# Instance norm in 3D on one core: three 64 KiB slots loaded, then three stored, in turn on one queue, with a two-pass variance split over the engines

## Chip, cores, metric

One Trainium2 chip (trn2), one of its cores. The metric is device time in microseconds (us), the median of several runs. The profile comes from one execution; its span is about 1.7 us shorter than the timed run (1249.7 against about 1251.5 us before).

Engines are named as the profile names them: PE is TensorE, DVE is VectorE, ACT is ScalarE, POOL is GpSimd, SP is SyncE. SP does no arithmetic here: it issues every load and store, one after another.

## The reference

```python
batch, channels, d, h, w = 8, 64, 32, 64, 64        # x is drawn from a standard normal, float32
def reference(x, eps):                              # eps = 1e-5
    mean = np.mean(x, axis=(2, 3, 4), keepdims=True)
    var = np.var(x, axis=(2, 3, 4), keepdims=True)
    return ((x - mean) / np.sqrt(var + eps)).astype(np.float32)
```

There are 512 instances of 131,072 elements. The kernel has to read 268.44 MB and write 268.44 MB; each element needs a statistic first and a multiply and an add afterwards.

## The kernel before

A tile holds 8 instances, each over 16 partitions, so 128 partitions x 8192 columns (32 KiB a partition, 4 MiB). Four such tiles exist. Statistics take one pass: DVE sums the values while ACT sums the squares. A small matmul adds up the 16 partitions of each instance. The normalise is split over three engines, in place.

```python
LAG = 2
data_pool = ctx.enter_context(tc.tile_pool(name="data", bufs=4))
# ... cut
norm_splits = [(nc.vector, 0, c1), (nc.scalar, c1, c2), (nc.gpsimd, c2, F)]   # c1 = F // 8, c2 = F // 4
# ... cut: in issue_compute, for each tile
nc.vector.reduce_sum(out=psums[:, k, 0:1], in_=x_tiles[:, k, :], axis=mybir.AxisListType.X)
nc.scalar.activation(out=sq_scratch, in_=x_tiles[:, k, :],
                     func=mybir.ActivationFunctionType.Square, accum_out=psums[:, k, 1:2])
# ... cut: matmul, mean, E[x^2] - mean^2, sqrt, reciprocal, bias, then the three normalise pieces
pending = {}
for g in range(n_groups):
    x_tiles = issue_load(g)
    issue_compute(g, x_tiles)
    pending[g] = x_tiles
    if g >= LAG:
        issue_store(g - LAG, pending.pop(g - LAG))
for g in range(n_groups - LAG, n_groups):
    issue_store(g, pending.pop(g))
```

Loads and stores therefore alternate in SP's program, and store g-2 stands behind load g.

Of the kernel before, what the change touches and what calls it, by code (L numbers as in the profile page):

```python
# [1 line left out]

# [4 lines left out]


@with_exitstack
def kernel(  # L10
    ctx: ExitStack,
    tc: tile.TileContext,
    x: bass.AP,
    eps: bass.AP,
    out: bass.AP,
):
    nc = tc.nc
    fp32 = mybir.dt.float32

    P = 128  # L20
    B, C, D, H, W = x.shape
    n_inst = B * C
    n_elem = D * H * W

    eps_f = float(eps)

    SPLIT = 16
    IPT = P // SPLIT
    F = n_elem // SPLIT

    G = 8
    KPG = G // IPT
    n_groups = n_inst // G

    LAG = 2

    x_packed = x.rearrange("b c d h w -> (b c) (d h w)").rearrange(
        "(k i) (s f) -> k (i s) f", i=IPT, s=SPLIT
    )
    out_packed = out.rearrange("b c d h w -> (b c) (d h w)").rearrange(  # L40
        "(k i) (s f) -> k (i s) f", i=IPT, s=SPLIT
    )

    singles = ctx.enter_context(tc.tile_pool(name="singles", bufs=1))
    data_pool = ctx.enter_context(tc.tile_pool(name="data", bufs=4))
    scratch_pool = ctx.enter_context(tc.tile_pool(name="scratch", bufs=2))
    stat_pool = ctx.enter_context(tc.tile_pool(name="stats", bufs=4))
    psum_pool = ctx.enter_context(tc.tile_pool(name="psum", bufs=4, space=bass.MemoryType.PSUM))

    ones_t = singles.tile([P, P], fp32)  # L50
    nc.vector.memset(ones_t, 1.0 / SPLIT)  # L51
    blk_pattern = [[-SPLIT, P // SPLIT], [0, SPLIT]]
    nc.gpsimd.affine_select(  # L53
        out=ones_t,
        in_=ones_t,
        pattern=blk_pattern,
        compare_op=mybir.AluOpType.is_ge,
        fill=0.0,
        base=0,
        channel_multiplier=1,  # L60
    )
    nc.gpsimd.affine_select(  # L62
        out=ones_t,
        in_=ones_t,
        pattern=[[SPLIT, P // SPLIT], [0, SPLIT]],
        compare_op=mybir.AluOpType.is_ge,
        fill=0.0,
        base=SPLIT - 1,
        channel_multiplier=-1,
    )  # L70

    inv_F = 1.0 / F

    c1 = F // 8
    c2 = F // 4
    norm_splits = [
        (nc.vector, 0, c1),
        (nc.scalar, c1, c2),
        (nc.gpsimd, c2, F),
    ]  # L80

    def issue_load(g):
        x_tiles = data_pool.tile([P, KPG, F], fp32, name="x_tiles")
        src = x_packed[g * KPG : (g + 1) * KPG].rearrange("k p f -> p k f")
        nc.sync.dma_start(out=x_tiles, in_=src)
        return x_tiles

    def issue_compute(g, x_tiles):
        psums = stat_pool.tile([P, KPG, 2], fp32, name="psums")

        for k in range(KPG):
            nc.vector.reduce_sum(  # L92
                out=psums[:, k, 0:1],
                in_=x_tiles[:, k, :],
                axis=mybir.AxisListType.X,
            )
            sq_scratch = scratch_pool.tile(
                [P, F], mybir.dt.bfloat16, name="sq_scratch"
            )
            nc.scalar.activation(  # L100
                out=sq_scratch,
                in_=x_tiles[:, k, :],
                func=mybir.ActivationFunctionType.Square,
                accum_out=psums[:, k, 1:2],
            )

        tot = psum_pool.tile([P, KPG, 2], fp32, name="tot")
        nc.tensor.matmul(  # L108
            out=tot,
            lhsT=ones_t,  # L110
            rhs=psums,
            start=True,
            stop=True,
        )

        me2 = stat_pool.tile([P, KPG, 2], fp32, name="me2")
        nc.vector.tensor_scalar(  # L117
            out=me2,
            in0=tot,
            scalar1=inv_F,  # L120
            scalar2=None,
            op0=mybir.AluOpType.mult,
        )
        mean = me2[:, :, 0]
        e2 = me2[:, :, 1]

        msq = stat_pool.tile([P, KPG], fp32, name="msq")
        nc.vector.tensor_mul(out=msq, in0=mean, in1=mean)  # L128

        var_eps = stat_pool.tile([P, KPG], fp32, name="var_eps")  # L130
        nc.vector.scalar_tensor_tensor(  # L131
            out=var_eps,
            in0=e2,
            scalar=eps_f,
            in1=msq,
            op0=mybir.AluOpType.add,
            op1=mybir.AluOpType.subtract,
        )

        std = stat_pool.tile([P, KPG], fp32, name="std")  # L140
        nc.scalar.activation(  # L141
            out=std,
            in_=var_eps,
            func=mybir.ActivationFunctionType.Sqrt,
        )
        scale = stat_pool.tile([P, KPG], fp32, name="scale")
        nc.vector.reciprocal(out=scale, in_=std)  # L147
        bias = stat_pool.tile([P, KPG], fp32, name="bias")
        nc.vector.scalar_tensor_tensor(  # L149
            out=bias,  # L150
            in0=mean,
            scalar=-1.0,
            in1=scale,
            op0=mybir.AluOpType.mult,
            op1=mybir.AluOpType.mult,
        )

        for k in range(KPG):
            for eng, lo, hi in norm_splits:
                if eng is nc.scalar:  # L160
                    nc.scalar.activation(  # L161
                        out=x_tiles[:, k, lo:hi],
                        in_=x_tiles[:, k, lo:hi],
                        func=mybir.ActivationFunctionType.Identity,
                        scale=scale[:, k : k + 1],
                        bias=bias[:, k : k + 1],
                    )
                else:
                    eng.tensor_scalar(  # L169
                        out=x_tiles[:, k, lo:hi],  # L170
                        in0=x_tiles[:, k, lo:hi],
                        scalar1=scale[:, k : k + 1],
                        scalar2=bias[:, k : k + 1],
                        op0=mybir.AluOpType.mult,
                        op1=mybir.AluOpType.add,
                    )

    def issue_store(g, x_tiles):
        dst = out_packed[g * KPG : (g + 1) * KPG].rearrange("k p f -> p k f")
        nc.sync.dma_start(out=dst, in_=x_tiles)  # L180

    pending = {}
    for g in range(n_groups):
        x_tiles = issue_load(g)
        issue_compute(g, x_tiles)
        pending[g] = x_tiles
        if g >= LAG:
            issue_store(g - LAG, pending.pop(g - LAG))
    for g in range(n_groups - LAG, n_groups):
        issue_store(g, pending.pop(g))  # L190


# [1 line left out]
_INS = ['x', 'eps']  # L194
_OUTS = [((8, 64, 32, 64, 64), 'float32')]
#: Inputs that are plain numbers.
_NUMBERS = {'eps': 9.999999747378752e-06}


# [26 lines left out]
```

## Time and profile before

| what | before |
|---|---|
| time, median of the first three runs (range) | 1251.46 us (1250.81 to 1252.0) |
| span of the profile | 1249.7 us |
| DMA queue's share of 16 engines' span; mean rate | 99.7%; 430 GB/s |
| busiest compute engine | DVE, 53% |
| DMA data packets (trace) | 16,384 of 32 KiB; median 1.213 us each |

First the page's engine line (busy us, share of the span, instruction count), its row of DMA shares in 40 slices of 31 us with the GB/s below it, and the line of the DMA queue (packets, MB, share of 16 engines). Read the digits as tenths of full occupation.

```profile
PE 35.7 (3%) x128; PEld 32.1 (3%) x128; DVE 659.2 (53%) x449; ACT 550.6 (44%) x258; POOL 380.3 (30%) x70
DMA  9999999999999999999999999999999999999998
GB/s 403 417 434 434 427 433 430 432 435 430 429 432 434 432 435 429 434 433 434 434 431 433 431 434 434 435 430 432 434 433 436 429 433 434 433 434 435 429 433 357
q1 hardware_dynamic: 18432, 536.88, 99.7%
```

No slice but the last falls below 9, and no compute engine is over 53%: the DMA engines bound this kernel from end to end. The Trainium skill ("DMA: Bandwidth & Descriptors", section "Where 436 GB/s comes from") gives 435 GB/s as the ceiling of the 16 ports through which the DMA engines reach on-chip memory; the slices, at 427 to 436 from the third to the last but one, agree. The same section goes on to say that transfers between the chip's main memory (HBM) and on-chip memory are held to about 358 GB/s; this trace does not agree: one core alone moved 430 GB/s in the mean. A saving in compute is worth nothing here, and compute that delays a transfer costs its whole delay.

The durations used for costing come from the page's groups of instructions (line, engine, operation, tile and shape, count | total busy us, mean ns of one | idle time before, and what ended it):

```profile
L92 DVE TENSOR_REDUCE psums<-x_tiles 128x1 f32<-128x8192 f32 x64 | 555.9, 8686 | 492.9 <-DMA x_tiles<-in_x_dram 492.9
L100 ACT ACTIVATE sq_scratch<-x_tiles 128x8192 bf16<-128x8192 f32 x64 | 449.9, 7029 | 461.3 <-DMA x_tiles<-in_x_dram 461.3
L169 POOL TENSOR_SCALAR x_tiles<-x_tiles,scale,bias 128x6144 f32<-128x6144 f32 x64 | 379.4, 5929 | 855.4 <-DVE bias L149 634.4
L161 ACT ACTIVATE x_tiles<-x_tiles,bias,scale 128x1024 f32<-128x1024 f32 x64 | 79.4, 1241 | 40.5 <-DVE bias L149 40.5
L169 DVE TENSOR_SCALAR x_tiles<-x_tiles,scale,bias 128x1024 f32<-128x1024 f32 x64 | 52.1, 813 | 2.5
```

DVE and ACT sit idle about 490 and 460 us in front of their statistics, waiting for loads: that is what slack looks like in a DMA-bound kernel.

One detail needs the instructions in order of time (start us, duration us, engine, line, operation). It shows how DVE's and POOL's shares of one normalise stand to each other:

```profile
1191.83 0.81 DVE L169 TENSOR_SCALAR x_tiles<-x_tiles,scale,bias 128x1024 f32<-128x1024 f32 x1
1192.04 5.93 POOL L169 TENSOR_SCALAR x_tiles<-x_tiles,scale,bias 128x6144 f32<-128x6144 f32 x1 [13.43 <-DVE bias L149]
...
1211.18 0.81 DVE L169 TENSOR_SCALAR x_tiles<-x_tiles,scale,bias 128x1024 f32<-128x1024 f32 x1
...
1211.70 5.63 POOL L169 TENSOR_SCALAR x_tiles<-x_tiles,scale,bias 128x6144 f32<-128x6144 f32 x1 [13.72 <-DVE bias L149]
```

POOL starts at different distances from DVE's start (0.21 and 0.52 us) and has different durations, but it ends 5.33 and 5.34 us after DVE *ends* (1191.83 + 0.81 = 1192.64, and 1192.04 + 5.93 = 1197.97). So POOL's work really begins when DVE's is over. The skill says the same ("SBUF — State Buffer", section "Who interferes with whom": a DVE instruction in a two-port mode, which takes the ports that the two engines share, and a GpSimd instruction exclude each other for the whole instruction). In this kernel it is harmless. When sizes change it has to be costed as a sum, not as a maximum.

### The profile page before, as it was taken

How to read it: one execution, taken by the hardware profiler on the slowest of the kernel's cores; microseconds unless marked ns; L12 is line 12 of the kernel's file. 1: busy time of each engine (PE TensorE's matmuls, PEld its weight loads, DVE VectorE, ACT ScalarE, POOL GpSimd, SP SyncE). 2: the span in 40 equal slices, each digit the busy share in tenths (PEclk: the TensorE clock that was granted, in tenths of full speed). 3: DMA queues.
4: the chain of work that ended last, by engine and by line, in shares of the span. 5: the costliest groups of instructions: out<-in, count | busy, mean ns of one | idle time of the engine just before them, and what ended most of it. 6: DMA issues, size and time to landing. Idle time of an engine off the chain costs nothing.

```text
span 1249.7 us, 1827 instructions
## 1 busy us (share of the span) xinstructions
PE 35.7 (3%) x128; PEld 32.1 (3%) x128; DVE 659.2 (53%) x449; ACT 550.6 (44%) x258; POOL 380.3 (30%) x70
## 2 busy tenths in 40 slices
PE   0000000000000000000000000000000000000000
PEld 0000000000000000000000000000000000000000
DVE  5736455464554645546546455464554645646543
ACT  5535445354453544535435344354453544534432
POOL 2332332313323233232331322313323233132231
DMA  9999999999999999999999999999999999999998
GB/s 403 417 434 434 427 433 430 432 435 430 429 432 434 432 435 429 434 433 434 434 431 433 431 434 434 435 430 432 434 433 436 429 433 434 433 434 435 429 433 357
DMA packets 18444, 536.99 MB, mean 430 GB/s; under 512 B 2048, under 2 KB 2048, under 8 KB 2048
## 3 DMA queue, kind: packets, MB, share of 16 engines
q1 hardware_dynamic: 18432, 536.88, 99.7%
q14 instruction: 11, 0.09, 0.0%
q8 instruction: 1, 0.02, 0.0%
HBM read 268.44 MB, written 268.44 MB: 430 GB/s over the span
## 4 chain that ended last, share of the span: by engine, by line
DMA 74%; issue 16%; POOL 7%; DVE 1%; POOLq 1%; PE 0%; ACT 0%
DMA out_dram<-x_tiles 39%; DMA x_tiles<-in_x_dram 35%; POOL x_tiles L169 7%; DVE psums L92 1%; POOLq L221 0%; DVE x_tiles L169 0%; POOLq L169 0%; PE tot L108 0%; ACT std L141 0%; DVE scale L147 0%; DVE msq L128 0%; DVE me L117 0%; DVE bias L149 0%; DVE var_eps L131 0%
## 5 line engine op out<-in xcount | busy, mean ns | idle before, releaser
L92 DVE TENSOR_REDUCE psums<-x_tiles 128x1 f32<-128x8192 f32 x64 | 555.9, 8686 | 492.9 <-DMA x_tiles<-in_x_dram 492.9
L100 ACT ACTIVATE sq_scratch<-x_tiles 128x8192 bf16<-128x8192 f32 x64 | 449.9, 7029 | 461.3 <-DMA x_tiles<-in_x_dram 461.3
L169 POOL TENSOR_SCALAR x_tiles<-x_tiles,scale,bias 128x6144 f32<-128x6144 f32 x64 | 379.4, 5929 | 855.4 <-DVE bias L149 634.4
L161 ACT ACTIVATE x_tiles<-x_tiles,bias,scale 128x1024 f32<-128x1024 f32 x64 | 79.4, 1241 | 40.5 <-DVE bias L149 40.5
L141 ACT ACTIVATE std<-var_eps 128x1 f32<-128x1 f32 x64 | 13.0, 203 | 178.7 <-DVE var_eps L131 178.7
L108 PE MATMUL tot<-psums,ones_t 128*128 128x2 f32 x128 | 35.7, 348 | 1193.5 <-DVE psums L92 1193.5
L108 PEld LDWEIGHTS tot<-psums,ones_t 128*128 128x128 f32 x128 | 32.1, 311 | 1197.1 <-issue 1197.1
L169 DVE TENSOR_SCALAR x_tiles<-x_tiles,scale,bias 128x1024 f32<-128x1024 f32 x64 | 52.1, 813 | 2.5
L117 DVE TENSOR_SCALAR me<-tot 128x2 f32<-128x2 f32 x64 | 10.2, 160 | 47.5 <-PE tot L108 47.5
L147 DVE RECIPROCAL scale<-std 128x1 f32<-128x1 f32 x64 | 10.5, 164 | 21.8 <-ACT std L141 21.8
L100 ACT ACTIVATION_READ_ACCUMULATOR sq_scratch<-x_tiles 128x1 f32 x64 | 11.9, 187 | 0.0
L128 DVE TENSOR_TENSOR msq<-me 128x1 f32<-128x1 f32 x64 | 10.2, 159 | 2.2
L131 DVE SCALAR_TENSOR_TENSOR var_eps<-me,msq 128x1 f32<-128x1 f32 x64 | 10.2, 159 | 2.2
L149 DVE SCALAR_TENSOR_TENSOR bias<-me,scale 128x1 f32<-128x1 f32 x64 | 10.2, 159 | 2.2
L100 ACT ACT_TABLE_LOAD x1 | 1.3, 1283 | 0.8 <-PEq L207 0.8
L141 ACT ACT_TABLE_LOAD x1 | 1.3, 1283 | 0.0
L51 DVE MEMSET ones_t<- 128x128 f32 x1 | 0.2, 165 | 0.9 <-PEq L207 0.9
L53 POOL TENSOR_SCALAR_AFFINE_SELECT ones_t<-ones_t 128x128 f32<-128x128 f32 x1 | 0.3, 343 | 0.6 <-DVE ones_t L51 0.6
L62 POOL TENSOR_SCALAR_AFFINE_SELECT ones_t<-ones_t 128x128 f32<-128x128 f32 x1 | 0.3, 338 | 0.1
L207 POOL MEMSET const-float32-0.0<- 128x1 f32 x1 | 0.1, 98 | 0.3 <-issue 0.3
L207 POOL MEMSET const-bfloat16-1.0<- 128x1 bf16 x1 | 0.1, 101 | 0.0
L207 POOL MEMSET const-uint8-127<- 128x1 uint8 x1 | 0.1, 101 | 0.0
(1 smaller groups left out, 0.1 us busy)
## 6 DMA issues: line engine op xcount, KB each, us to landing
x_tiles<-in_x_dram SPq DMA_DIRECT2D x64, 4096.0 KB, 29.0
out_dram<-x_tiles SPq DMA_DIRECT2D x64, 4096.0 KB, 31.5
```

Of the source, the lines that this page charges most:

```text
L92: nc.vector.reduce_sum(out=psums[:, k, 0:1], in_=x_tiles[:, k, :], axis=mybir.AxisListType.X,)
L100: nc.scalar.activation(out=sq_scratch, in_=x_tiles[:, k, :], func=mybir.ActivationFunctionType.Square, accum_out=psums[:, k, 1:2],)
L108: nc.tensor.matmul(out=tot, lhsT=ones_t, rhs=psums, start=True, stop=True,)
L117: nc.vector.tensor_scalar(out=me2, in0=tot, scalar1=inv_F, scalar2=None, op0=mybir.AluOpType.mult,)
L128: nc.vector.tensor_mul(out=msq, in0=mean, in1=mean)
L131: nc.vector.scalar_tensor_tensor(out=var_eps, in0=e2, scalar=eps_f, in1=msq, op0=mybir.AluOpType.add, op1=mybir.AluOpType.subtract,)
L141: nc.scalar.activation(out=std, in_=var_eps, func=mybir.ActivationFunctionType.Sqrt,)
L147: nc.vector.reciprocal(out=scale, in_=std)
L149: nc.vector.scalar_tensor_tensor(out=bias, in0=mean, scalar=-1.0, in1=scale, op0=mybir.AluOpType.mult, op1=mybir.AluOpType.mult,)
L161: nc.scalar.activation(out=x_tiles[:, k, lo:hi], in_=x_tiles[:, k, lo:hi], func=mybir.ActivationFunctionType.Identity, scale=scale[:, k : ...
L169: eng.tensor_scalar(out=x_tiles[:, k, lo:hi], in0=x_tiles[:, k, lo:hi], scalar1=scale[:, k : k + 1], scalar2=bias[:, k : k + 1], op0=mybir ...
L207: nc = _bacc.Bacc("TRN2", target_bir_lowering=False, num_devices=1)
```

## The change

The intent: bigger packets (64 KiB rows), transfers of one direction batched (three loads, then three stores), and a numerically safer variance (mean first, then the squares of x - mean), with the added pass spread over the engines. The data now lies in three slots of 128 x 16384 (8 MiB each, 24 MiB in all) instead of four of 4 MiB (16 MiB). The first two slots are loaded and stored in halves, so that work can begin early.

```diff
+    SLOTS = 3
+    COLS = 16384
+    BIG = P * COLS // n_elem        # 16 instances a slot
+    HALF = BIG // 2
# ... cut
+    def compute(t, n):
+        avg = avgs[n]
+        width = t.shape[1]
+        cut = width * 5 // 8
+        sums = stat_pool.tile([P, 2], fp32, name="sums")
+        nc.vector.reduce_sum(out=sums[:, 0:1], in_=t[:, :cut], axis=mybir.AxisListType.X)
+        accumulate(t[:, cut:], Act.Identity, 0.0, sums[:, 1:2])      # ACT sums the other 3/8
+        mean_ps = averaged(avg, sums, "mean_ps")
+        neg_mean = stat_pool.tile([P, 1], fp32, name="neg_mean")
+        nc.vector.tensor_scalar(out=neg_mean, in0=mean_ps, scalar1=-1.0, scalar2=None, op0=Alu.mult)
+        squares = stat_pool.tile([P, 2], fp32, name="squares")
+        used = accumulate(t, Act.Square, neg_mean, squares)          # 2 pieces of 8192 on ACT
+        var_ps = averaged(avg, squares[:, :used], "var_ps")
# ... cut: sqrt on ACT, reciprocal and bias on DVE
+        half, rest = width // 2, width * 3 // 4
+        nc.scalar.activation(out=t[:, rest:], in_=t[:, rest:], func=Act.Identity, scale=scale, bias=bias)
+        for engine, lo, hi in ((nc.gpsimd, 0, half), (nc.vector, half, rest)):
+            engine.tensor_scalar(out=t[:, lo:hi], in0=t[:, lo:hi], scalar1=scale, scalar2=bias,
+                                 op0=Alu.mult, op1=Alu.add)
# ... cut
+    loaded, stored = 0, 0
+    while stored < n_slots:
+        load_and_compute(range(loaded, min(stored + SLOTS, n_slots)))
+        loaded = min(stored + SLOTS, n_slots)
+        turn = first_turn if stored == 0 else SLOTS
+        for g in range(stored, stored + turn):
+            for part in work.pop(g):
+                store(*part)
+        stored += turn
```

The diff does not show how ACT's instructions of different slots end up interleaved; the built program does. In a full turn of slots a, b, c, ACT runs: sum a, squares a, **sum b**, sqrt a, normalise a, squares b, **sum c**, sqrt b, normalise b, squares c, sqrt c, normalise c.

More of the change, by code (lines that the diff above doesn't have):

```diff
@@ L4 @@
 import concourse.tile as tile
-from concourse import bass_utils, mybir
+from concourse import mybir
 from concourse._compat import with_exitstack
@@ L18 @@
     fp32 = mybir.dt.float32
+    Alu = mybir.AluOpType
+    Act = mybir.ActivationFunctionType
     P = 128
@@ L25 @@
     eps_f = float(eps)
-    SPLIT = 16
-    IPT = P // SPLIT
-    F = n_elem // SPLIT
-    G = 8
-    KPG = G // IPT
-    n_groups = n_inst // G
-    LAG = 2
-    x_packed = x.rearrange("b c d h w -> (b c) (d h w)").rearrange(
-        "(k i) (s f) -> k (i s) f", i=IPT, s=SPLIT
-    )
-    out_packed = out.rearrange("b c d h w -> (b c) (d h w)").rearrange(
-        "(k i) (s f) -> k (i s) f", i=IPT, s=SPLIT
-    )
-    singles = ctx.enter_context(tc.tile_pool(name="singles", bufs=1))
-    data_pool = ctx.enter_context(tc.tile_pool(name="data", bufs=4))
@@ L46 @@
-    scratch_pool = ctx.enter_context(tc.tile_pool(name="scratch", bufs=2))
-    stat_pool = ctx.enter_context(tc.tile_pool(name="stats", bufs=4))
-    psum_pool = ctx.enter_context(tc.tile_pool(name="psum", bufs=4, space=bass.MemoryType.PSUM))
-    ones_t = singles.tile([P, P], fp32)
-    nc.vector.memset(ones_t, 1.0 / SPLIT)
-    blk_pattern = [[-SPLIT, P // SPLIT], [0, SPLIT]]
-    nc.gpsimd.affine_select(
-        out=ones_t,
-        in_=ones_t,
-        pattern=blk_pattern,
-        compare_op=mybir.AluOpType.is_ge,
-        fill=0.0,
-        base=0,
-        channel_multiplier=1,
-    )
@@ L62 @@
-    nc.gpsimd.affine_select(
-        out=ones_t,
-        in_=ones_t,
-        pattern=[[SPLIT, P // SPLIT], [0, SPLIT]],
-        compare_op=mybir.AluOpType.is_ge,
-        fill=0.0,
-        base=SPLIT - 1,
-        channel_multiplier=-1,
-    )
-    inv_F = 1.0 / F
-    c1 = F // 8
-    c2 = F // 4
-    norm_splits = [
-        (nc.vector, 0, c1),
-        (nc.scalar, c1, c2),
-        (nc.gpsimd, c2, F),
-    ]
-    def issue_load(g):
-        x_tiles = data_pool.tile([P, KPG, F], fp32, name="x_tiles")
-        src = x_packed[g * KPG : (g + 1) * KPG].rearrange("k p f -> p k f")
-        nc.sync.dma_start(out=x_tiles, in_=src)
-        return x_tiles
@@ L88, in issue_compute @@
-    def issue_compute(g, x_tiles):
-        psums = stat_pool.tile([P, KPG, 2], fp32, name="psums")
-        for k in range(KPG):
-            nc.vector.reduce_sum(
-                out=psums[:, k, 0:1],
-                in_=x_tiles[:, k, :],
-                axis=mybir.AxisListType.X,
-            )
-            sq_scratch = scratch_pool.tile(
-                [P, F], mybir.dt.bfloat16, name="sq_scratch"
-            )
-            nc.scalar.activation(
-                out=sq_scratch,
-                in_=x_tiles[:, k, :],
-                func=mybir.ActivationFunctionType.Square,
-                accum_out=psums[:, k, 1:2],
-            )
-        tot = psum_pool.tile([P, KPG, 2], fp32, name="tot")
-        nc.tensor.matmul(
-            out=tot,
-            lhsT=ones_t,
-            rhs=psums,
-            start=True,
-            stop=True,
-        )
-        me2 = stat_pool.tile([P, KPG, 2], fp32, name="me2")
-        nc.vector.tensor_scalar(
-            out=me2,
-            in0=tot,
-            scalar1=inv_F,
-            scalar2=None,
-            op0=mybir.AluOpType.mult,
-        )
-        mean = me2[:, :, 0]
-        e2 = me2[:, :, 1]
-        msq = stat_pool.tile([P, KPG], fp32, name="msq")
-        nc.vector.tensor_mul(out=msq, in0=mean, in1=mean)
-        var_eps = stat_pool.tile([P, KPG], fp32, name="var_eps")
-        nc.vector.scalar_tensor_tensor(
-            out=var_eps,
-            in0=e2,
-            scalar=eps_f,
-            in1=msq,
-            op0=mybir.AluOpType.add,
-            op1=mybir.AluOpType.subtract,
-        )
-        std = stat_pool.tile([P, KPG], fp32, name="std")
-        nc.scalar.activation(
-            out=std,
-            in_=var_eps,
-            func=mybir.ActivationFunctionType.Sqrt,
-        )
-        scale = stat_pool.tile([P, KPG], fp32, name="scale")
-        nc.vector.reciprocal(out=scale, in_=std)
-        bias = stat_pool.tile([P, KPG], fp32, name="bias")
-        nc.vector.scalar_tensor_tensor(
-            out=bias,
-            in0=mean,
-            scalar=-1.0,
-            in1=scale,
-            op0=mybir.AluOpType.mult,
-            op1=mybir.AluOpType.mult,
-        )
-        for k in range(KPG):
-            for eng, lo, hi in norm_splits:
-                if eng is nc.scalar:
-                    nc.scalar.activation(
-                        out=x_tiles[:, k, lo:hi],
-                        in_=x_tiles[:, k, lo:hi],
-                        func=mybir.ActivationFunctionType.Identity,
-                        scale=scale[:, k : k + 1],
-                        bias=bias[:, k : k + 1],
-                    )
-                else:
-                    eng.tensor_scalar(
-                        out=x_tiles[:, k, lo:hi],
-                        in0=x_tiles[:, k, lo:hi],
-                        scalar1=scale[:, k : k + 1],
-                        scalar2=bias[:, k : k + 1],
-                        op0=mybir.AluOpType.mult,
-                        op1=mybir.AluOpType.add,
-                    )
@@ L178, in issue_store @@
-    def issue_store(g, x_tiles):
-        dst = out_packed[g * KPG : (g + 1) * KPG].rearrange("k p f -> p k f")
-        nc.sync.dma_start(out=dst, in_=x_tiles)
-    pending = {}
-    for g in range(n_groups):
-        x_tiles = issue_load(g)
-        issue_compute(g, x_tiles)
-        pending[g] = x_tiles
-        if g >= LAG:
-            issue_store(g - LAG, pending.pop(g - LAG))
-    for g in range(n_groups - LAG, n_groups):
-        issue_store(g, pending.pop(g))
+    SLOTS = 3
+    COLS = 16384
@@ new lines, with averaging @@
+    BIG = P * COLS // n_elem
+    HALF = BIG // 2
+    x_f = x.rearrange("b c d h w -> (b c) (d h w)")
+    out_f = out.rearrange("b c d h w -> (b c) (d h w)")
+    singles = ctx.enter_context(tc.tile_pool(name="singles", bufs=1))
+    data_pool = ctx.enter_context(tc.tile_pool(name="data", bufs=SLOTS))
+    stat_pool = ctx.enter_context(tc.tile_pool(name="stats", bufs=4))
+    psum_pool = ctx.enter_context(
+        tc.tile_pool(name="psum", bufs=2, space=bass.MemoryType.PSUM)
+    )
+    def averaging(split):
+        avg = singles.tile([P, P], fp32, name=f"avg{split}")
+        nc.vector.memset(avg, 1.0 / n_elem)
+        nc.gpsimd.affine_select(
+            out=avg,
+            in_=avg,
+            pattern=[[-split, P // split], [0, split]],
+            compare_op=Alu.is_ge,
+            fill=0.0,
+            base=0,
+            channel_multiplier=1,
+        )
+        nc.gpsimd.affine_select(
+            out=avg,
+            in_=avg,
+            pattern=[[split, P // split], [0, split]],
+            compare_op=Alu.is_ge,
+            fill=0.0,
+            base=split - 1,
+            channel_multiplier=-1,
+        )
+        return avg
@@ new lines, with rows, load, store @@
+    avgs = {n: averaging(P // n) for n in (HALF, BIG)}
+    eps_t = singles.tile([P, 1], fp32, name="eps_t")
+    nc.vector.memset(eps_t, eps_f)
+    unused = singles.tile([P, COLS // 2], mybir.dt.uint8, name="unused")
+    def rows(ap, first, n):
+        return ap[first : first + n].rearrange("i (s f) -> (i s) f", s=P // n)
+    def load(t, first, n):
+        nc.sync.dma_start(out=t, in_=rows(x_f, first, n))
+    def store(t, first, n):
+        nc.sync.dma_start(out=rows(out_f, first, n), in_=t)
@@ new lines, in accumulate, with averaged @@
+    def accumulate(t, func, bias, to):
+        width = t.shape[1]
+        pieces = -(-width // unused.shape[1])
+        step = width // pieces
+        for k in range(pieces):
+            nc.scalar.activation(
+                out=unused[:, :step],
+                in_=t[:, k * step : (k + 1) * step],
+                func=func,
+                bias=bias,
+                accum_out=to[:, k : k + 1],
+            )
+        return pieces
+    def averaged(avg, parts, name):
+        ps = psum_pool.tile([P, 1], fp32, name=name)
+        n = parts.shape[1]
+        for k in range(n):
+            nc.tensor.matmul(
+                out=ps,
+                lhsT=avg,
+                rhs=parts[:, k : k + 1],
+                start=k == 0,
+                stop=k == n - 1,
+            )
+        return ps
@@ new lines, in compute @@
+    def compute(t, n):
+        avg = avgs[n]
+        width = t.shape[1]
+        cut = width * 5 // 8
+        sums = stat_pool.tile([P, 2], fp32, name="sums")
+        nc.vector.reduce_sum(
+            out=sums[:, 0:1], in_=t[:, :cut], axis=mybir.AxisListType.X
+        )
+        accumulate(t[:, cut:], Act.Identity, 0.0, sums[:, 1:2])
+        mean_ps = averaged(avg, sums, "mean_ps")
+        neg_mean = stat_pool.tile([P, 1], fp32, name="neg_mean")
+        nc.vector.tensor_scalar(
+            out=neg_mean, in0=mean_ps, scalar1=-1.0, scalar2=None, op0=Alu.mult
+        )
+        squares = stat_pool.tile([P, 2], fp32, name="squares")
+        used = accumulate(t, Act.Square, neg_mean, squares)
+        var_ps = averaged(avg, squares[:, :used], "var_ps")
+        std = stat_pool.tile([P, 1], fp32, name="std")
+        nc.scalar.activation(out=std, in_=var_ps, func=Act.Sqrt, bias=eps_t)
+        scale = stat_pool.tile([P, 1], fp32, name="scale")
+        nc.vector.reciprocal(out=scale, in_=std)
+        bias = stat_pool.tile([P, 1], fp32, name="bias")
+        nc.vector.tensor_mul(out=bias, in0=neg_mean, in1=scale)
+        half, rest = width // 2, width * 3 // 4
+        nc.scalar.activation(
+            out=t[:, rest:], in_=t[:, rest:], func=Act.Identity, scale=scale, bias=bias
+        )
+        for engine, lo, hi in ((nc.gpsimd, 0, half), (nc.vector, half, rest)):
+            engine.tensor_scalar(
+                out=t[:, lo:hi],
+                in0=t[:, lo:hi],
+                scalar1=scale,
+                scalar2=bias,
+                op0=Alu.mult,
+                op1=Alu.add,
+            )
@@ new lines, with load_and_compute @@
+    n_slots = n_inst // BIG
+    first_turn = n_slots % SLOTS or SLOTS
+    work = {}
+    def load_and_compute(group):
+        for g in group:
+            t = data_pool.tile([P, COLS], fp32, name="xt")
+            if g < first_turn:
+                cut = COLS // 2
+                work[g] = [
+                    (t[:, :cut], g * BIG, HALF),
+                    (t[:, cut:], g * BIG + HALF, HALF),
+                ]
+            else:
+                work[g] = [(t, g * BIG, BIG)]
+            for part in work[g]:
+                load(*part)
+        for g in group:
+            for t, _, n in work[g]:
+                compute(t, n)
```

## The prediction

> **What bounds the kernel now.** The DMA engines. The DMA queue table gives q1 99.7% of 16 engines' span, 430 GB/s mean. The trace's DMA packets: 16,384 of 32 KiB, 1.213 us each in both directions (also in the all-load start and the all-store tail), so 1024 x 1.213 = 1242 us per engine. The busiest compute engine, DVE, is at 53%. The Trainium skill ("DMA: Bandwidth & Descriptors", "Where 436 GB/s comes from") puts the ceiling at 435 GB/s; the trace agrees. Bytes do not change, so the floor stays 536.9 MB / 435 = 1234 us.
>
> **What the change can save.** If a 64 KiB row is one packet, half the packets at about 8 ns overhead each: about 4 us. Batching directions saves nothing: packets take the same in both. No-bubble time: about 1243.
>
> **What it costs.** Before, loads and stores alternate, compute well ahead of the store. Now SP issues L L L, S S S per turn. A store waits for its compute, and no load can be queued meanwhile (SP is in order, all three slots are full). An 8 MiB transfer takes about 19.35 us, so after the first load of a turn lands (t=0) its store is due at 38.4, the next at 58, the third at 77.
>
> Durations scaled from the instruction groups of before: reduce of 10240 on DVE 10.8 (8.69 for 8192); ACT partial sum of 6144 5.5; squares 2 x 7.4 (7.03 + 0.19 accumulator read + 0.2 bias operand); ACT normalise of 4096 3.8; matmul pairs 0.7 to 1.3; sqrt, reciprocal, bias 0.65. Normalise: DVE 2.4, then POOL 7.05: before, each POOL normalise ends 5.34 us after DVE's, whenever it started. The skill agrees ("SBUF — State Buffer", "Who interferes with whom": DVE in a 2-port mode and GpSimd exclude each other). So 9.5.
>
> The built order on ACT is: sum a, squares a, sum b, sqrt a, normalise a, squares b, sum c, sqrt b, normalise b, squares c, sqrt c. Hence:
> - a: mean at 12.2, squares to 27.2, sum b to 32.7, bias 33.4, normalised 43.0. Due 38.4; with 0.85 us from issue to first packet (last store of before): gap 5.5.
> - b: squares 37.2 to 52.0, sum c to 57.5, normalised 67.9; first packet 68.7, store a ended 63.2: gap 5.5.
> - c: squares 62.0 to 76.8, normalised 87.7; store b ends 88.1: gap about 0.4.
>
> About 11.4 us of idle DMA per turn, on the critical path because the DMA queue is empty then. Nine full turns give 103 us; the first, short turn about 6, its half stores being hidden behind the third load. 1243 + 103 + 6, about 1350 us.
>
> **Prediction: 1350 us, 80% range 1325 to 1375; faster 0.01, same 0.05, slower 0.94.**
>
> **What would show each step.** Packets about 9,500, of 64 KiB, 2.42 us each. DMA queue share about 92%, mean about 398 GB/s; slices dip twice per turn, between last load and first store and between first and second store. SP's waits: stores on POOL or DVE normalise for 4 to 5 us after the DMA ran dry. The chain of waits goes through ACT squares and sums instead of DMA alone. ACT busy about 780 us, DVE about 450.
>
> **What would make it wrong.** DVE and POOL normalising side by side (only gap a shrinks; ACT sets b); sum b not delaying sqrt a; pure-direction phases moving faster than 435 GB/s, which no stretch of the trace shows; extra semaphore waits between ACT's squares (slower).

## The result

| what | before | after |
|---|---|---|
| time, median of 4 runs (range) | 1251.73 us (1250.81 to 1252.65) | 1351.16 us (1351.05 to 1351.32) |
| ratio, 95% interval | | 1.0795 (1.0779 to 1.081): slower |
| span of the profile | 1249.7 us | 1349.6 us |
| DMA queue's share; mean rate | 99.7%; 430 GB/s | 92.7%; 398 GB/s |
| 16 DMA engines idle between first and last packet, mean of the engines | 4.2 us | 97.0 us |
| packets' own time, per engine | 1245.3 us | 1250.8 us |
| of which slow packets, per engine | 3.2 us | 12.5 us |

Ratios are the mean time of one kernel's fast runs over that of the other's of the same rounds, so not quite the ratio of the medians. The last three rows are worked out from the start and duration of every DMA packet in the trace: idle is the time in which fewer than 16 packets are in flight, weighted by the missing ones; slow packets are the sum of what each packet takes beyond the median of its size (1.213 us for 32 KiB, 2.418 us for 64 KiB), divided by 16.

The change costs 99.4 us (1351.16 - 1251.73). In the profiled pair, whose spans differ by 99.9 us, engine idle time accounts for 92.8 and the packets' own time for 5.5; the last 2 us I don't attribute.

The same lines of the page as before; the slices are 34 us long here:

```profile
PE 73.8 (5%) x264; PEld 64.5 (5%) x264; DVE 453.1 (34%) x173; ACT 764.7 (57%) x266; POOL 295.2 (22%) x42
DMA  9999899889988998899799889988998899699979
GB/s 404 422 448 435 373 404 435 373 373 404 435 373 373 421 429 361 373 435 435 305 410 435 373 373 404 435 373 373 404 435 373 371 435 431 286 435 412 396 342 404
q1 hardware_dynamic: 9792, 536.88, 92.7%
```

The busiest compute engine, ACT, is at 57%. By this line alone everything would still be hidden behind the DMA. But the DMA row now has 7s and 8s (and one 6) all the way along, and the GB/s row falls to 373 or below twice in nearly every turn, that is in about two slices of four. The average of busy time says nothing about *when* ACT is busy.

The groups that answer to those of before. A line's mean may mix two shapes: these are the views by shape, so it doesn't.

```profile
L88 ACT ACTIVATE unused<-xt,neg_mean 128x8192 uint8<-128x8192 f32 x64 | 455.5, 7117 | 78.7 <-DVE neg_mean L122 77.7
L116 DVE TENSOR_REDUCE sums<-xt 128x1 f32<-128x10240 f32 x30 | 324.6, 10820 | 551.9 <-DMA xt<-in_x_dram 551.9
L139 POOL TENSOR_SCALAR xt<-xt,scale,bias 128x8192 f32<-128x8192 f32 x30 | 276.4, 9214 | 978.3 <-DVE bias L133 856.0 <-ACT std L129 75.9 <-DVE neg_mean L122 46.4
L88 ACT ACTIVATE unused<-xt 128x6144 uint8<-128x6144 f32 x30 | 159.7, 5323 | 441.4 <-DMA xt<-in_x_dram 440.8
L135 ACT ACTIVATE xt<-xt,bias,scale 128x4096 f32<-128x4096 f32 x30 | 114.1, 3802 | 15.6 <-issue 9.4 <-DVE bias L133 6.2
```

POOL's mean of 9.2 us for 8192 columns is not its speed: in most of these instructions the first 2.4 us are a wait for DVE.

Now one full turn in order of time. Slot a lands at 732.40, b at 751.75, c at about 771.

```profile
732.40 5.32 ACT L88 ACTIVATE unused<-xt 128x6144 uint8<-128x6144 f32 x1 [46.74 <-DMA xt<-in_x_dram]
732.40 10.82 DVE L116 TENSOR_REDUCE sums<-xt 128x1 f32<-128x10240 f32 x1 [48.21 <-DMA xt<-in_x_dram]
...
744.57 7.12 ACT L88 ACTIVATE unused<-xt,neg_mean 128x8192 uint8<-128x8192 f32 x1 [6.76 <-DVE neg_mean L122]
...
751.82 7.12 ACT L88 ACTIVATE unused<-xt,neg_mean 128x8192 uint8<-128x8192 f32 x1
...
759.07 5.33 ACT L88 ACTIVATE unused<-xt 128x6144 uint8<-128x6144 f32 x1
...
764.39 0.24 ACT L129 ACTIVATE std<-var_ps,eps_t 128x1 f32<-128x1 f32 x1
...
765.27 2.41 DVE L139 TENSOR_SCALAR xt<-xt,scale,bias 128x4096 f32<-128x4096 f32 x1
765.27 9.29 POOL L139 TENSOR_SCALAR xt<-xt,scale,bias 128x8192 f32<-128x8192 f32 x1 [74.04 <-DVE bias L133]
768.82 7.11 ACT L88 ACTIVATE unused<-xt,neg_mean 128x8192 uint8<-128x8192 f32 x1
...
774.59 44.14 SPq L80 DMA_DIRECT2D out_dram<-xt  x3
...
789.50 9.29 POOL L139 TENSOR_SCALAR xt<-xt,scale,bias 128x8192 f32<-128x8192 f32 x1 [14.94 <-DVE bias L133]
...
809.06 9.30 POOL L139 TENSOR_SCALAR xt<-xt,scale,bias 128x8192 f32<-128x8192 f32 x1 [10.28 <-DVE bias L133]
818.77 1.38 SPq L77 DMA_DIRECT2D xt<-in_x_dram  x2
```

Store a is issued at 774.59, as soon as POOL's normalise of a has ended (765.27 + 9.29 = 774.56): 42.2 us after a landed. The squares of a ended at 758.9; the square root ran only at 764.39, because slot b's partial sum (759.07) stood before it on ACT. The issue line of the three stores covers 44 us because SP stands inside it, waiting for slots b and c (ready at 798.79 and 818.36). Until SP is through, the next load can't be queued. By about 795 store a has left the DMA engines, but the load that would refill slot a stands behind stores b and c on SP. Whether loads issued from another engine would fill gap b, no run tested.

What the DMA does meanwhile, by windows of the same turn (window, its length, then busy us of PE, PEld, DVE, ACT, POOL, the clock, the DMA share and GB/s):

```profile
732.40:771.00 38.60, 3.36 (x12) 2.93 (x12) 24.65 (x7) 31.30 (x11) 5.73 (x1) 1.00 0.94 407
771.00:775.20 4.20, 0.00 (x0) 0.00 (x0) 4.11 (x1) 4.20 (x1) 3.56 (x1) 1.00 0.00 0
775.20:795.00 19.80, 2.19 (x8) 1.93 (x8) 9.56 (x5) 19.26 (x9) 5.50 (x1) 1.00 0.98 424
795.00:799.50 4.50, 0.00 (x0) 0.00 (x0) 0.00 (x0) 4.50 (x1) 3.79 (x1) 1.00 0.00 0
799.50:819.00 19.50, 1.18 (x4) 1.01 (x4) 2.73 (x3) 12.02 (x6) 9.30 (x1) 1.00 1.00 430
819.00:858.60 39.60, 0.00 (x0) 0.00 (x0) 0.00 (x0) 0.00 (x0) 0.00 (x0) 1.00 1.00 424
```

In two stretches the DMA is at 0.00 while ACT is busy the whole time (4.20 of 4.20, 4.50 of 4.50). In the last stretch, 39.6 us of stores and loads, no compute engine does anything: the slack of this kernel exists, but it comes after the work that needed it. From the packets, engine idle time is about 5.0 us between the last load and store a, 4.8 us between stores a and b, and 0.2 us between b and c; 9.95 us a turn. Nine full turns give 89.6 us, the short first turn 5.1 us.

SP's own waits in the changed kernel mislead a little (who waited for what: total us, times, longest):

```profile
SPq L80 <- DVE xt L139: 880.8, 33, 54.5
SPq L77 <- DMA out_dram<-xt: 212.2, 21, 20.1
SPq L80 <- POOL xt L139: 167.7, 31, 5.7
```

Stores wait 881 us "for DVE". Most of that is harmless waiting while transfers are queued, and DVE is named only for the wait that came last before POOL's. The total of a wait says nothing about its cost; what counts is whether the DMA queue was empty at its end. The chain of waits is of no help in this profile: it follows the work back only to 1298 us of 1349.6.

### The profile page after: what moved, and what is told of

Read it like the earlier page. It is cut to its first block, busy times and chain, and to the rows that moved or that the text cites. A ratio compares the mean times of both kernels' runs of the same rounds, so it can differ in the third digit from the quotient of the medians.

```text
span 1349.6 us, 1391 instructions
## 1 busy us (share of the span) xinstructions
PE 73.8 (5%) x264; PEld 64.5 (5%) x264; DVE 453.1 (34%) x173; ACT 764.7 (57%) x266; POOL 295.2 (22%) x42
## 2 busy tenths in 40 slices
DMA packets 9801, 536.97 MB, mean 398 GB/s; under 512 B 1088, under 2 KB 1088, under 8 KB 1088
## 3 DMA queue, kind: packets, MB, share of 16 engines
q1 hardware_dynamic: 9792, 536.88, 92.7%
## 5 line engine op out<-in xcount | busy, mean ns | idle before, releaser
L116 DVE TENSOR_REDUCE sums<-xt 128x1 f32<-128x10240 f32 (+1 forms) x34 | 346.5, 10192 | 566.7 <-DMA xt<-in_x_dram 566.7
L139 POOL TENSOR_SCALAR xt<-xt,scale,bias 128x8192 f32<-128x8192 f32 (+1 forms) x34 | 293.6, 8636 | 1031.6 <-DVE bias L133 879.6
L88 ACT ACTIVATE unused<-xt,neg_mean 128x8192 uint8<-128x8192 f32 x64 | 455.5, 7117 | 78.7 <-DVE neg_mean L122 77.7
L88 ACT ACTIVATE unused<-xt 128x6144 uint8<-128x6144 f32 (+1 forms) x34 | 170.8, 5022 | 452.5 <-DMA xt<-in_x_dram 451.9
L135 ACT ACTIVATE xt<-xt,bias,scale 128x4096 f32<-128x4096 f32 (+1 forms) x34 | 122.4, 3601 | 17.4 <-issue 9.4
L139 DVE TENSOR_SCALAR xt<-xt,scale,bias 128x4096 f32<-128x4096 f32 (+1 forms) x34 | 91.3, 2685 | 1.4 <-DVE bias L133 0.5
L102 PE MATMUL mean_ps<-sums,avg 128*128 128x1 f32 x136 | 37.7, 358 | 715.9 <-DVE sums L116 658.6
L102 PEld LDWEIGHTS mean_ps<-sums,avg 128*128 128x128 f32 x136 | 33.6, 318 | 719.7 <-DVE sums L116 628.8
L102 PE MATMUL var_ps<-squares,avg 128*128 128x1 f32 x128 | 37.5, 362 | 527.8 <-ACT unused L88 527.8
L102 PEld LDWEIGHTS var_ps<-squares,avg 128*128 128x128 f32 x128 | 32.1, 311 | 533.3 <-ACT unused L88 533.3
```

Source lines behind the costliest of these rows:

```text
L88: nc.scalar.activation(out=unused[:, :step], in_=t[:, k * step : (k + 1) * step], func=func, bias=bias, accum_out=to[:, k : k + 1],)
L102: nc.tensor.matmul(out=ps, lhsT=avg, rhs=parts[:, k : k + 1], start=k == 0, stop=k == n - 1,)
L116: nc.vector.reduce_sum(out=sums[:, 0:1], in_=t[:, :cut], axis=mybir.AxisListType.X)
L135: nc.scalar.activation(out=t[:, rest:], in_=t[:, rest:], func=Act.Identity, scale=scale, bias=bias)
L139: engine.tensor_scalar(out=t[:, lo:hi], in0=t[:, lo:hi], scalar1=scale, scalar2=bias, op0=Alu.mult, op1=Alu.add,)
```

## The experiments

The main theory: in a turn the three loads are in flight or landed in all three slots, so nothing can be queued until store a is ready. Stores a, b, c fall due at fixed times (about 38, 58 and 77 us after a lands), but the compute chain, which has ACT working almost without a break, makes a and b late. So it is the *combination* of turns with a long chain. The rival explanations are: (A) turns of one direction, or 64 KiB packets, make the DMA itself slower; (B) the two-pass statistics are more work than this kernel can hide; (C) the end of the chain, the normalise on POOL and DVE, sets it alone; (D) the sum of b that stands before a's square root sets it. (The expectation of e5 uses the letter C for a variant: DVE and POOL not excluding each other.)

Summary first. "Idle" and "slow packets" are computed as above, from each run's trace, in us per engine. (The expectations count slow packets of 64 KiB alone: 11.7 in the changed kernel, 18.0 in e2, 2.6 in e4, 13.8 in e9.)

| run | time, median (range) us | ratio to before (95%) | idle | slow packets |
|---|---|---|---|---|
| after | 1351.16 (1351.05 to 1351.32) | 1.0795 (1.0779 to 1.081) | 97.0 | 12.5 |
| e1_onepass | 1249.05 (1248.81 to 1249.08) | 0.9981 (0.9966 to 0.9996) | 3.3 | 4.2 |
| e2_alternate | 1270.21 (1269.38 to 1271.14) | 1.0151 (1.0136 to 1.0166) | 8.3 | 19.8 |
| e3_copy_turns | 1247.70 (1247.19 to 1248.57) | 0.9972 (0.9957 to 0.9986) | 2.4 | 3.5 |
| e4_copy_alternate | 1249.96 (1249.18 to 1251.33) | 0.9990 (0.9974 to 1.0007) | 3.8 | 4.2 |
| e5_norm_no_pool | 1323.04 (1323.02 to 1323.16) | 1.0571 (1.0558 to 1.0585) | 69.7 | 11.5 |
| e6_norm_dve_only | 1313.57 (1313.4 to 1313.77) | 1.0496 (1.0482 to 1.0509) | 60.7 | 11.2 |
| e7_act_in_order | 1408.90 (1408.78 to 1408.94) | 1.1257 (1.1241 to 1.1273) | 155.1 | 12.1 |
| e8_alternate_onepass | 1250.78 (1248.2 to 1254.21) | 0.9995 (0.9981 to 1.0009) | 6.1 | 6.6 |
| e9_alternate_no_pool | 1261.89 (1261.49 to 1263.45) | 1.0076 (1.0059 to 1.0093) | 4.4 | 15.5 |
| e10_six_slots | 1252.04 (1251.47 to 1252.66) | 0.9998 (0.9982 to 1.0015) | 5.5 | 3.1 |

All diffs are against the changed kernel unless another is named.

### e1_onepass: the turns kept, the statistics put back to one pass

```diff
-        nc.vector.reduce_sum(out=sums[:, 0:1], in_=t[:, :cut], axis=mybir.AxisListType.X)
-        accumulate(t[:, cut:], Act.Identity, 0.0, sums[:, 1:2])
+        nc.vector.reduce_sum(out=sums, in_=t, axis=mybir.AxisListType.X)
# ... cut here and below: the tiles
+        used = accumulate(t, Act.Square, 0.0, squares)
+        e2_ps = averaged(avg, squares[:, :used], "var_ps")
# ... cut: mean and neg_mean as before
-        used = accumulate(t, Act.Square, neg_mean, squares)
-        var_ps = averaged(avg, squares[:, :used], "var_ps")
+        nc.vector.tensor_mul(out=msq, in0=neg_mean, in1=neg_mean)
+        nc.vector.tensor_sub(out=var_ps, in0=e2_ps, in1=msq)
```

> The changed kernel's loads, stores, slots and normalise, with only the statistics put back to one pass (DVE sums a whole slot, 17.3 us estimated; ACT squares beside it, 14.6 us). Main theory (stores come late because the compute chain of a turn is too long for three loads in, three stores out): slot a is ready 28.7 us after it lands (due 38.4), b at 50.5 (due 58), c at 72 (due 77), so no DMA gap is left: 1243 to 1253 us. Rival A (turns of one direction, or 64 KiB packets, slow the DMA itself): stays above 1320.

Measured: 1249.05 us, the gaps gone. The same windows of one turn (a lands at 683.6; then loads b and c, stores a, b, c, and the next load):

```profile
683.60:722.20 38.60, 2.93 (x10) 2.50 (x10) 37.34 (x8) 32.47 (x10) 9.30 (x1) 1.00 1.00 433
722.20:741.50 19.30, 1.18 (x4) 1.01 (x4) 18.06 (x8) 17.22 (x5) 9.30 (x1) 1.00 1.00 431
741.50:760.90 19.40, 1.18 (x4) 1.00 (x4) 5.71 (x7) 5.10 (x4) 9.30 (x1) 1.00 1.02 443
760.90:780.20 19.30, 0.00 (x0) 0.00 (x0) 0.00 (x0) 0.00 (x0) 0.00 (x0) 1.00 1.00 431
780.20:799.50 19.30, 0.00 (x0) 0.00 (x0) 0.00 (x0) 0.00 (x0) 0.00 (x0) 1.00 0.99 431
```

No window is below 0.99. DVE and ACT are just as concentrated at the front of the turn, but slot a is ready 28.7 us after landing (store issued at 712.36) instead of 42.2. So the turns themselves cost nothing if the chain is short enough: rival A falls. DVE does *more* here than in the changed kernel (654.5 against 453.1 us); what matters is not how busy an engine is but how long the chain is.

### e2_alternate: the two passes kept, loads and stores alternating

```diff
-            if g < first_turn:
+            if g < first_turn or g == n_slots - 1:
# ... cut: the loop over turns
+    for g in range(n_slots):
+        load_and_compute([g])
+        if g >= 1:
+            for part in work.pop(g - 1):
+                store(*part)
+    for part in work.pop(n_slots - 1):
+        store(*part)
```

> The changed kernel's compute untouched (two passes, same split), same three slots of 64 KiB, but load g+1 queued between store g-1 and store g; the last slot in halves like the first ones. Main theory: a store is due 38.7 us after its load lands and is ready 37.5 us after (42.2 in the changed kernel's trace less the 4.8 us that the next slot's sum delays it), and ACT needs 24 us of every 38.7: at most a few tenths of a us of gap a slot, 1243 to 1262 us. Rival B (two passes are simply more work than the kernel can hide, whatever the order): stays above 1320.

Measured: 1270.21 us, above the range that I gave, but 81 of the 99 us are back with the compute code untouched (only the last slot is now also worked in halves). Rival B, in its strong form, falls. The idle time, 8.3 us, is about what was expected. What I had not expected are 19.8 us of slow packets. They are taken up in e9 and e10.

### e3_copy_turns and e4_copy_alternate: the DMA alone

Wrong results: the compute is left out, so the kernels copy. (They passed the comparison all the same: with inputs of mean near 0 and variance near 1 the reference is nearly a copy, so it is a weak test of this kernel's arithmetic.)

```diff
-                compute(t, n)
+                pass
```

> Wrong result on purpose: the changed kernel's DMAs in the same order, no compute, so it copies. Measures the DMA's own time for three loads, three stores in turn. Main theory: 1241 to 1254 us (512 packets of 2.418 us an engine, 1238, and start and end), and the 11.7 us of slow packets of the changed kernel shrink if they come from restarts after a gap, stay if they come from the change of direction. Rival A: above 1300.

> Wrong result on purpose: the same copy with loads and stores of 8 MiB alternating. Main theory: 1240 to 1250 us, within 0.8% of e3_copy_turns. If batching directions helps the DMA, e3 is below this one; if it hurts, above.

Measured: 1247.70 and 1249.96 us. Turns are 0.2% quicker than alternation, with ranges that do not overlap in four runs each; whether direction or only the way the engines drift apart makes it was not tested. Both figures are floors: on this chip a pure copy is only 0.1 to 0.3% quicker than the kernel before, so with these orders of transfers no rearrangement of compute could have gained 2%. And the slow packets shrink to 3.5 us, so the change of direction alone makes few of them; nor does it make many together with compute, since e1, with turns and compute but a queue that stays full, has 4.2.

### e5_norm_no_pool: POOL's part of the normalise to DVE

```diff
-        for engine, lo, hi in ((nc.gpsimd, 0, half), (nc.vector, half, rest)):
+        for engine, lo, hi in ((nc.vector, 0, rest),):
```

> The changed kernel with POOL's half of the normalise given to DVE (DVE 12288 columns, estimated 6.7 us; ACT keeps 4096). In the changed kernel DVE's 2.41 us and POOL's half run one after the other, 9.5 us from bias to the end. Main theory: every store is ready 2.6 us earlier, slot b's too, which sets the turn; nine turns and the short one: 1351 less 25, about 1326 us (1318 to 1334), gap a about 2.4, gap b still about 4.8. If DVE and POOL did not exclude each other (rival C), ready times would not move by more than the difference of 7.1 and 6.7 us and the time would stay above 1344.

Measured: 1323.04 us, gap a 2.5 us, gap b 4.7 us. Slot a's normalise on DVE, in one piece:

```profile
750.81 6.68 DVE L139 TENSOR_SCALAR xt<-xt,scale,bias 128x12288 f32<-128x12288 f32 x1
```

*Taking an engine away* from the normalise makes the kernel 28 us faster, because DVE does 12288 columns in 6.68 us, while 4096 on DVE and then 8192 on POOL end 9.3 us after DVE's start. Gap b stays although slot b is ready earlier too, because store a starts and ends earlier by the same amount. The variant of rival C named in the expectation (above 1344 us) falls.

### e6_norm_dve_only: all of the normalise on DVE

```diff
-        nc.scalar.activation(
-            out=t[:, rest:], in_=t[:, rest:], func=Act.Identity, scale=scale, bias=bias
-        )
-        for engine, lo, hi in ((nc.gpsimd, 0, half), (nc.vector, half, rest)):
+        for engine, lo, hi in ((nc.vector, 0, width),):
```

> The changed kernel with all of the normalise on DVE (16384 columns, estimated 8.8 us): less parallel, but ACT is relieved of 3.8 us a slot. Main theory (ACT's chain up to slot b's square root sets the turn): slot b's squares start 3.4 us earlier and its store is ready 4.1 us earlier, so about 4.1 x 9.5 = 39 us less: 1312 us (1302 to 1322), gap b down to about 1.4, gap a still about 4.3. If the normalise tail alone set it (rival C): 0.7 us a turn, 1344 us.

Measured: 1313.57 us, gap a 4.6 us, gap b 1.4 us. The normalise itself is only 0.5 us quicker (8.81 against 9.3 us), so gap a hardly moves; but ACT has 3.8 us less to do, the squares of b start 3.5 us earlier, and most of b's gap closes. Rival C expected 1344. Together e5 and e6 say what sets a turn: the chain on ACT up to b's square root, plus the normalise of b.

### e7_act_in_order: ACT pinned to program order

Three calls on ACT (one of them serves the sums and the squares) are wrapped so that the scheduler may not move them past each other; sum b now comes after normalise a.

```diff
-        nc.scalar.activation(out=std, in_=var_ps, func=Act.Sqrt, bias=eps_t)
+        tc.keep_in_program_order(nc.scalar.activation(out=std, in_=var_ps, func=Act.Sqrt, bias=eps_t))
# ... cut: the same around the sums and squares, and around the normalise on ACT
```

> The changed kernel with ACT's instructions pinned to program order, so that slot b's partial sum no longer stands before slot a's square root. Main theory: slot a is ready about 2.3 us earlier (39.9 instead of 42.2; DVE's sum of b now holds its scale) and gap a falls to about 2.4, but slot b's squares start 4.5 us later and slot c's end about 6.6 us later: gaps about 2.4, 6.7 and 7.2 instead of 5.0, 4.8 and 0.2, and the kernel is slower, about 1410 us (1385 to 1425). If the delay of slot a's store by the sum of b were the cause (rival D, my prediction's wording taken at face value): faster, about 1330 us.

Measured: 1408.90 us; idle 2.9, 6.5 and 6.5 us a turn. In order of time, slot a landing at 760.52:

```profile
787.84 0.26 ACT L129 ACTIVATE std<-var_ps,eps_t 128x1 f32<-128x1 f32 x1 [0.68 <-PE var_ps L102]
790.60 0.15 DVE L131 RECIPROCAL scale<-std 128x1 f32<-128x1 f32 x1
...
791.20 9.30 POOL L139 TENSOR_SCALAR xt<-xt,scale,bias 128x8192 f32<-128x8192 f32 x1 [71.85 <-DVE bias L133]
794.83 5.31 ACT L88 ACTIVATE unused<-xt 128x6144 uint8<-128x6144 f32 x1
...
800.53 0.34 SPq L80 DMA_DIRECT2D out_dram<-xt  x1
```

Store a does go out earlier (40.0 us after landing instead of 42.2), and the kernel is 58 us slower. ACT waits 3 us for DVE, whose sum of b now holds up a's reciprocal, and the sum of b no longer fills ACT's wait; so b and c come later. Removing the delay that is visible at gap a is the wrong repair: rival D falls, and the order that the scheduler chose was the better one.

### e8_alternate_onepass: meant to beat both

e1's statistics and e2's loop.

> Three slots of 64 KiB, loads and stores alternating, first and last slots in halves, statistics in one pass: a version meant to beat both. Main theory: a store is ready 28.7 us after its load lands and due after 38.7, so no gap: 512 x 2.418 = 1238 us and about 4 us of start, end and slow packets: 1240 to 1247 us, 0.4 to 0.9% below the kernel before. If 64 KiB packets bring nothing on the critical path: 1249 to 1253.

Measured: 1250.78 us with a wide range (1248.2 to 1254.21); a miss, level with the kernel before. In the profiled run, the slowest of the six, 5.8 of its 6.1 us of idle time lie after 1240 us: some engines finish their last packets several us before others, and the time is that of the last one. In e2 and e9, whose queue runs dry along the way, only 0.2 and 0.7 us of idle time lie there (1.8 in the last 12 us of the kernel before, whose queue is always full too). So the likely reading is that with a queue always full nothing makes the engines wait for each other, and that the 4 us which 64 KiB packets save (below) are lost at the end; the quicker executions have no trace, so this is not shown for them. e1, at 0.9981 of before (0.9966 to 0.9996), is the one version that beat both kernels, by 0.2%, far below the 2% that would count as faster.

### e9_alternate_no_pool and e10_six_slots: what made the packets slow in e2

e9 is e2 with e5's edit. e10 keeps the two passes but cuts the same memory into six slots of 32 KiB:

```diff
-    SLOTS = 3
-    COLS = 16384
+    SLOTS = 6
+    COLS = 8192
+    LAG = 3
# ... cut: no halves; the loop of e2 with g >= LAG and store g - LAG, and the last LAG stores after it
```

> e2_alternate (two passes, loads and stores alternating) with POOL's half of the normalise on DVE, as in e5. In e2 each store was issued only when the load before it had run out on some of the 16 engines, and packets that start after such a moment were slow: 18 us per engine in the whole kernel, against 2.6 in the pure copy e4. Theory: what e2 lacked was a few tenths of a us of slack; here every store is ready 2.6 us earlier, the queue does not run dry, slow packets fall below 6 us and idle time of the engines before the end below 1 us: 1246 to 1255 us. If two passes themselves, or their traffic on the chip's memory, slowed the packets, it stays near 1268.

> The changed kernel's two-pass compute with six slots of 32 KiB instead of three of 64 (the same on-chip memory), loads and stores alternating, each store three loads behind. A store is due about 58 us after its load lands and ready about 21 us after, so several transfers are always queued. e9 left open whether its 14 us of slow packets came from two passes or from the queue still running dry on the engines that are ahead. Theory (too little queued): slow packets below 6 us an engine, time 1246 to 1255 us. If two passes slow the packets themselves: 1258 to 1268.

Measured: e9 1261.89 us with 15.5 us of slow packets, a miss: 2.6 us of slack are not enough. e10 1252.04 us with 3.1 us of slow packets, like the kernel before (3.2). So two passes, with ACT at 64% (its busiest in any run), cost nothing when several transfers are always queued; the slow packets went when the short queue did. e10 changes packet size, lag and slot count together, so which of these it was is not separated.

## Why the prediction was right

**Total.** Predicted 1350 (1325 to 1375), measured 1351.16. Part of that closeness is luck: two terms were off in opposite directions, by about 14 us (the gaps) and 10 us (the time without gaps).

**The bound and the ceiling: right.** Packets of 64 KiB take 2.418 us against 2 x 1.213 = 2.426 us, so 8 ns are saved for each: about 500 x 8 ns = 4 us an engine, as predicted. The pure copies show there was nothing else to win.

**The mechanism: right, and shown from both sides.** e1 keeps the turns and shortens the chain, e2 keeps the chain and drops the turns, and each gives back at least 81 of 99 us. The queue is empty in the trace at the two places named.

**The gaps: mis-sized by about 13%.** I put 5.5 + 5.5 + 0.4 = 11.4 us a turn; measured 5.0 + 4.8 + 0.2 = 9.95. Slot a was ready at 42.2, not 43.0, b at 66.4, not 67.9, c at 86.0, not 87.7 (each from the landing of a). The mis-sized terms are the squares (2 x 7.4 estimated; the two of a took 744.57 to 758.94, 14.4 us), ACT's sum (5.5 estimated, 5.32 measured), and POOL's part (7.05 estimated; it ends 774.56 - 767.68 = 6.88 us after DVE). In the squares about half of the difference is the bias operand: put at 0.2 us each, it cost 0.09 (7.117 us with it, 7.029 without). Over nine turns and the first one that is 94.7 us instead of 109.

**The time without gaps: mis-sized the other way.** I put 1243; it is 1349.6 - 97.0 = 1252.6. The missing term is 12.5 us of slow packets, against 3.2 before; the prediction's "packets take the same in both" does not hold for the last packets of such a batch. Wherever a load follows store c in a full turn, the last packets of store c took 3.1 to 3.2 us in the mean of the 16 engines instead of 2.42 (about 6.6 of the 12.5 us), the first load packets behind them 2.5 to 2.6, and the first store packets after a gap 2.46.

**The checks.** ACT 764.7 (780 predicted), DVE 453.1 (450), share 92.7% (92%), 398 GB/s (398), packets 9,801 (9,500; 7,680 of them are of 64 KiB, 1,024 of 32 KiB, most of the rest of 4 bytes). The chain of waits was to show ACT instead of DMA; its short tail names ACT, but it covers too little of the span to count. The dips show in the slices, but where both gaps of a turn fall into one slice (305 and 286 GB/s) only the windows separate them.

**What was left open.** Why the last packets of a store are slow in front of a load, when the queue has run dry shortly before, is not settled. That the 16 engines run nearly in step then does not explain it by itself. In the changed kernel they start those packets within 0.13 to 0.73 us of each other in all of these nine turns but one; in that one they are 1.7 us apart, and the packets are as slow (3.14 us). In e3, whose queue stays full, the engines are 0.7 to 2.3 us apart, and the packets in front of a load take no longer than usual. What goes with most of the slow packets is a queue that had run dry; how it makes them slow, no run shows. Nor is it the only condition: at e3's first change from loads to stores, with a full queue, the last load packets took 3.26 us in the mean.

## What to carry to other kernels

In a DMA-bound kernel, compare each store's *due time* with the time its data is ready, slot by slot through one whole turn; busy shares hide a miss completely (ACT was at 57% while the DMA stood still). Batching transfers by direction concentrates the deadlines and leaves no transfer to queue in the meantime, so it pays only if the whole chain, from a landing to the last normalise, fits into the transfers that are already queued. When a chain is late, shorten the resource that the *later* slots share; clearing the delay seen at the first gap can make the kernel slower, as e7 did by 58 us.

## What the Trainium skill lacked or had wrong

- "DMA: Bandwidth & Descriptors": it has nothing on what an emptied queue costs beyond the fixed time of a transfer. Here, after the queue had run dry, the last packets of a batch of stores, in front of a load, took 3.1 to 3.2 us in the mean instead of 2.42, and slow packets added up to 12.5 us an engine (19.8 in e2), against 3.5 in a copy whose queue stayed full.
- The same page, "Where 436 GB/s comes from": its limit of about 358 GB/s for transfers with HBM, given there without a condition, does not hold for one core alone (430 GB/s here). The page's own note on its measured rates ties that figure to both cores of a pair streaming; no run here tried that.
- The same page, "Why small descriptors are slow (HBM only)": it puts the fixed overhead at about 3 cycles a packet, besides 32 bytes of descriptor metadata. At the 850 MHz of its bandwidth section the 3 cycles are 3.5 ns (an estimate); two 32 KiB packets take 8 ns longer than one of 64 KiB, so all that a packet costs here is about twice that. How much of it is the metadata, no run shows.
- The same page does not say that the engines can finish far apart, so that the last ones set the time: in the profiled run of e8, whose queue stayed full, 5.8 us of idle time lie in the last 12 us of the profile, against 0.7 in e9, whose queue ran dry along the way.
- "SBUF — State Buffer", "Who interferes with whom": right, and worth a number for planning. 4096 columns on DVE and then 8192 on POOL end 9.3 us after DVE's start; DVE alone does all 12288 in 6.68 us.
